# Two transformer blocks on one core: an expert weight ring that begins in the mixer's buffers, and a reordered head

## The chip, the cores and the metric

The kernel runs on one core of one Trainium2 chip, in one launch. The metric is the device time of that launch in microseconds, as a median of several runs. The engines are named as the profile names them: PE (TensorE, matrix multiplies), DVE (VectorE), ACT (ScalarE), POOL (GpSimd) and SP (SyncE, which here only issues DMAs).

## The reference

256 tokens of width 1024 (float32) and 256 context tokens go through two blocks.

```python
def adaln(cvec, w, b):                       # six vectors of 1024: shift, scale, gate, twice
    m = silu(cvec) @ w + b
    return split(m, 6)

# first block
x = x + sincos_2d(256)
hc = rms_norm(ctx, norm1_g) * (1 + csc1) + csh1
s_f, s_b = context_states(hc @ w_in[:, 512:2048])           # final states of gated linear attention
hx = rms_norm(x, norm1_g) * (1 + sc1) + sh1
x = x + gt1 * token_mixer(hx @ w_in, s_f, s_b)              # attention branch, convolution branch, merge
h = rms_norm(x, norm2_g) * (1 + sc2) + sh2
x = x + gt2 * hier_moe(h)        # 4 groups x 8 experts (1024 -> 512 -> 1024, gate and up), top 1 group, top 2 experts
x = rms_norm(x, final_norm_g)
# second block, two layers, each
hx, hc = modulate(rms_norm(x), adaln(c_2)), modulate(rms_norm(ctx_2), adaln(c_ctx_2))
# ... retention and gated linear attention over both, an MLP of 4096, each with a gate
```

All weights are float32 in HBM. The 32 experts alone are 201 MB (32 x 3 matrices of 1024 x 512).

## The kernel before, in words

The kernel is written in a tile framework: the program order sets priorities, a planner puts each engine's instructions into one fixed order by a cost model, and a tile's buffer is handed to the next tile of the same tag when its last reader is done. Each engine runs its own list in order. Weight loads all go through SP's one DMA queue, so a load that waits for its buffer holds back all loads behind it.

*Precision.* Most products are made from high and low halves: `split` (lines 204 to 217) loads a chunk of weights into a buffer "raw" (three in the pool `wp`), ACT rounds it into a "whi" buffer, DVE writes the rest into a "wlo" buffer (two of each), and `mm3` (lines 223 to 228) makes three matmuls.

*Head* (lines 551 to 580). `params_c` turns the two condition vectors into columns and applies silu. The shift of adaLN (columns 0 to 1023) is made on DVE by `ada`, with multiply-adds over 512 columns for both vectors (line 289). The scale (columns 1024 to 2047) is made on PE by `ada_pe`, with the vectors as the stationary operand, two output rows, and then transposes (lines 261 to 269). Both are generators and run in turns; each turn loads a 1 MB chunk, `ada` into the two "wlo" buffers, `ada_pe` into "raw". `params0` packs small parameters as rows of one tile `prow`, with DMAs that alternate between ACT's and SP's queues, and turns them. The context tokens are loaded at the third turn, transposed, and their sums of squares made on PE (`stats`, line 322). Then two chunks of `w_in` are split and the tokens x are loaded, transposed and summed. `norm_mod` writes the modulated, split activations `hh` and `hl` (lines 366 to 371), which the first projection (the values, lines 583 to 591) reads.

*Mixer* (lines 660 to 955). Chunks of 256 columns of `w_in` are projected by `proj`; between them `tick` runs pieces of the block's other adaLN vectors on DVE. `hg_pair` does two heads of the attention branch, twice; at each head it calls `next(pieces)`, one of the four pieces of the second block's adaLN shift (`ada_pe`, line 654). The filter of the convolution branch (`hyena_filter`) is issued on ACT after the instruction `early`, which is the square root of the context's statistics. The small loads of the router's weights (lines 858 to 864) go out on ACT's queue in the head.

*End of the mixer* (lines 956 to 1002). The tags h0 and h1 of the pool `xp` are free once the last projection has read `hh` and `hl`. Two loads of 2 MB go into them: the second block's adaLN scale (`adaw`). At the last chunk of `w_out` the first three expert chunks go into the "raw" buffers.

*Router and experts* (`moe`). `ada_pe` makes the second block's scale from `adaw` in pieces: one ahead of the router's chain on DVE, two ahead of the branch, the last ahead of the first experts. A branch (`tc.If(most > CAP)`, line 1163) guards a fallback for an expert with more than 64 tokens, which is not taken here. Expert weights come in 192 chunks of 1 MB through a ring of 14 buffers (`chunk`): three "raw" of `wp`, three "raw" of `pm`, two "whi", two "wlo", and four halves of h0 and h1. The first ten are loaded ahead of the branch, the four in h0 and h1 behind it. For each quad of experts tokens are gathered by matmuls with a selection tile (line 1234), then for pairs of experts come gate and up (line 1271), down (line 1301) and the weighted sum back (line 1319).

Of the kernel before, what the change touches and what calls it, by code (L numbers as in the profile page):

```python
# [26 lines left out]
def _consts():  # L27

    if CONSTS:
# [5 lines left out]
        [np.eye(P), np.tile((np.arange(24) == 15)[None], (P, 1)), np.tile(np.arange(8)[None], (P, 1))], 1).astype(f32)  # L35
# [87 lines left out]
class K:  # L123


    def __init__(self, nc, tc, I, out, cap=64, dbg=None):
# [13 lines left out]
        self.kres = self.cp.tile([P, 160], F32, name="kres")  # L140
        nc_.scalar.dma_start(self.kres, I["k_res"])
        self.ident = self.kres[:, 0:128]
        self.hot = self.kres[:, 128:160]
        self.ones = self.cp.tile([P, 256], F32, name="ones")
# [86 lines left out]
    def param_pack(self, i, rows, pool, eng):  # L231
# [14 lines left out]
    def ada_pe(self, pool, w, col0, s16, fin, got=()):  # L246

        nc = self.nc
        sv = s16.rearrange("p (i k) -> p k i", i=2)
        m = pool.tile([P, 16], F32, tag="adam", name="adam")  # L250
        for c in range(2):
            pt = self.mm()
            for q in range(2):
                if got:
                    v = got[c][:, 4 * q:4 * q + 4]
                else:
                    v = self.raw(w[512 * q:512 * q + 512, col0 + 512 * c:col0 + 512 * c + 512]
                                 .rearrange("(k p) c -> p k c", p=P))
                for kk in range(4):
                    k = 4 * q + kk  # L260
# [8 lines left out]
            nc.vector.tensor_copy(m.rearrange("p (i j) -> p j i", i=2)[:, 4 * c:4 * c + 4], p2[:, :, :2])  # L269
            yield  # L270
        fin(m)
# [128 lines left out]
def params_c(s, pool):  # L400
# [8 lines left out]
    nc.scalar.activation(s.sc, pt[:, :16], AF.Silu)  # L409


def params0(s, pool):
# [6 lines left out]
        (r(I["hy_d"][0]), 4), (r(I["hy_conv_b"][0]), 12)], pool, nc.scalar)  # L419
# [7 lines left out]
def params(s, pool):  # L427
# [10 lines left out]
    nc.scalar.activation(s.sc2, p1[:, 76:92], AF.Silu)  # L438
    s.cvw = p1[:, 0:36]
# [93 lines left out]
def block1_mixer(s):  # L533
    nc, tc, I = s.nc, s.tc, s.I
    mt = nc.tensor.matmul
    with tc.tile_pool(name="p1", bufs=1) as pool_:
        pool = Pool(pool_, {"b8": 5, "b4": 3, "s4": 4, "t2": 6, "sq": 3,
                            "etot": 2, "adam": 2},
                    {"rstd": "s4", "nt": "sq", "prow": "sqo", "adarow": "sqo"})
# [104 lines left out]
        pieces = s.ada_pe(pool, I["ada_w_2"][0], 0, s.sc2, fin0)  # L644
# [33 lines left out]
        def hg_pair(hp):  # L678
# [11 lines left out]
            for j in range(2):  # L690
                next(pieces, None)
# [166 lines left out]
        nc.scalar.dma_start(s.wr[:, :, 0:4], I["moe_router_g_w"][0].rearrange("(k p) g -> p k g", p=P))  # L858
        for g in range(4):
            nc.scalar.dma_start(s.wr[:, :, 4 + 8 * g:12 + 8 * g],  # L860
                                I["moe_router_e_w"][0, g].rearrange("(k p) e -> p k e", p=P))
        s.rb = s.cp.tile([P, 36], F32, name="rb")
        nc.scalar.dma_start(s.rb[:, 0:4], I["moe_router_g_b"].broadcast_to([P, 4]))
        nc.scalar.dma_start(s.rb[:, 4:36], I["moe_router_e_b"].rearrange("o g e -> o (g e)").broadcast_to([P, 32]))
# [91 lines left out]
        s.adaw = []  # L956
        for c in range(2):
            v = s.xp.tile([P, 8, 512], F32, tag=f"h{1 - c}", name="adaw")
# [1003 lines left out]
```

## Time and profile before

| | |
|---|---|
| time, median of 3 runs | 2000.6 us (2000.2 to 2002.79) |
| the profiled execution's own time | 2003.38 us |
| its span, first to last instruction | 2001.6 us |
| PE / DVE / ACT busy | 1925.4 / 1099.4 / 676.7 us |
| mean granted TensorE clock | 0.981 of full speed |
| moved by DMA | 426.18 MB, mean 213 GB/s |

The span can be read in stages: the head up to the first projection matmul, the mixer up to about 400 us, router and experts up to about 890 us, the second block up to the end. "Busy" of PE is modelled for pipelined matmuls, so a full PE can still be a slow one. A granted clock of 1.00 is 2.4 GHz, 0.50 is 1.2 GHz.

### The profile page before, as it was taken

Reading aid. Unit: us, or ns where it says so; the run is one execution under the profiler, and the core shown is the slowest. Engines: PE = TensorE matmul, PEld = TensorE weight load, DVE = VectorE, ACT = ScalarE, POOL = GpSimd, SP = SyncE. Lnnn points to the kernel's source line nnn. Section 1 sums busy time; section 2 is a strip of 40 time slices with the busy share of each in tenths; the row PEclk is TensorE's granted clock in tenths of the full one; section 3 lists DMA queues with packets and bytes.
Section 4 is the critical chain, followed back from the end, with each engine's and each line's share of the span. In section 5 each row is a group of like instructions: output and inputs, shape, how many; then the busy total and the mean of one; then the engine's idle time right before and its main releaser. Section 6 shows DMA issues by size and latency. Waiting matters only on the chain.

```text
span 2001.6 us, 28164 instructions
## 1 busy us (share of the span) xinstructions
PE 1925.4 (96%) x11748; PEld 1438.7 (72%) x11748; DVE 1099.4 (55%) x2034; ACT 676.7 (34%) x991; POOL 6.1 (0%) x18
## 2 busy tenths in 40 slices
PE   6998999999999999989999999999999999999998
PEld 2856679944444444448888888778788968989998
DVE  5768796531111111125869858565534656887555
ACT  2564544421111111033432333231323444443444
POOL 0000000000000000000000000000000000000000
PEclk8999999999999999989999999999999989989999
DMA  8535537889999999973243523444323244457552
GB/s 282 174 107 192 167 127 239 288 356 421 421 421 421 421 421 421 421 271 110 67 147 127 170 64 128 152 141 147 126 84 106 56 137 148 157 180 232 187 176 101
DMA packets 217882, 426.18 MB, mean 213 GB/s; under 512 B 16171, under 2 KB 152392, under 8 KB 192920
## 3 DMA queue, kind: packets, MB, share of 16 engines
q1 hardware_dynamic: 208616, 419.75, 57.8%
q10 hardware_dynamic: 9008, 4.51, 0.8%
q8 instruction: 94, 1.54, 0.3%
q14 instruction: 36, 0.29, 0.0%
q0 software_dynamic: 128, 0.08, 0.0%
HBM read 423.26 MB, written 1.05 MB: 212 GB/s over the span
## 4 chain that ended last, share of the span: by engine, by line
PE 68%; DVE 4%; DMA 4%; ACT 2%; issue 0%; DVEq 0%; ACTq 0%; SPq 0%
PE mm L226 14%; PE mm L228 14%; PE mm L227 14%; PE mm L1271 10%; PE mm L1301 3%; PE at L1301 3%; DMA raw<-in_moe_w_down_dram 2%; PE at L1234 2%; PE at L1319 1%; PE tr L296 1%; DVE wlo L216 1%; DMA raw<-in_moe_w_up_dram 1%; DMA rawh<-in_moe_w_gate_dram 1%; DVE acc L289 1%; ACT whi L215 1%; PE at L1712 1%
## 5 line engine op out<-in xcount | busy, mean ns | idle before, releaser
L226 PE MATMUL mm<-hh,whi 128*128 128x256 f32 (+2 forms) x1232 | 411.4, 334 | 6.0 <-DVE sq L1890 2.4
L228 PE MATMUL mm<-hh,wlo 128*128 128x256 f32 (+2 forms) x1232 | 406.1, 330 | 8.7 <-DVE wlo L216 8.7
L227 PE MATMUL mm<-hl,whi 128*128 128x256 f32 (+2 forms) x1232 | 408.1, 331 | 0.1
L216 DVE TENSOR_TENSOR wlo<-raw,whi 128x2048 fp32r<-128x2048 f32 (+2 forms) x138 | 303.6, 2200 | 179.2 <-ACT whi L215 178.9
L215 ACT CAST whi<-raw 128x2048 fp32r<-128x2048 f32 (+2 forms) x138 | 253.1, 1834 | 359.5 <-PE mm L227 317.8
L226 PEld LDWEIGHTS mm<-hh,whi 128*128 128x128 f32 (+1 forms) x1232 | 236.2, 192 | 33.8 <-issue 5.0
L228 PEld LDWEIGHTS mm<-hh,wlo 128*128 128x128 f32 (+1 forms) x1232 | 236.2, 192 | 32.9 <-DVE wlo L216 10.0
L227 PEld LDWEIGHTS mm<-hl,whi 128*128 128x128 f32 (+1 forms) x1232 | 236.0, 192 | 25.4 <-issue 5.5
L289 DVE SCALAR_TENSOR_TENSOR acc<-raw,sc,acc 128x512 f32<-128x512 f32 x308 | 219.2, 744 | 15.3 <-DMA raw<-in_ada_w_dram 13.9
L226 PE MATMUL mm<-hidh,whi 128*128 128x256 f32 (+1 forms) x544 | 178.9, 331 | 0.0
L228 PE MATMUL mm<-hidh,wlo 128*128 128x256 f32 (+1 forms) x544 | 177.4, 329 | 0.1
L227 PE MATMUL mm<-hidl,whi 128*128 128x256 f32 (+1 forms) x544 | 177.2, 328 | 0.0
L1271 PE MATMUL mm<-raw,xg 128*64 128x512 f32 x736 | 172.5, 595 | 1.0 <-DMA raw<-in_moe_w_up_dram 1.0
L228 PE MATMUL mm<-whi,hl 128*128 128x256 f32 x512 | 148.6, 291 | 2.8 <-DVE hl L371 2.8
L226 PE MATMUL mm<-whi,hh 128*128 128x256 f32 x512 | 149.0, 292 | 2.2 <-ACT hh L370 1.3
L227 PE MATMUL mm<-wlo,hh 128*128 128x256 f32 x512 | 147.6, 288 | 0.0
L1271 PEld LDWEIGHTS mm<-raw,xg 128*64 128x64 f32 x736 | 54.6, 137 | 97.7 <-issue 93.0
L1279 DVE SCALAR_TENSOR_TENSOR glo<-mm,ws,glo 128x512 f32<-128x512 f32 x16 | 12.0, 751 | 190.2 <-PE mm L1271 168.2
L228 PEld LDWEIGHTS mm<-hidh,wlo 128*128 128x128 f32 x544 | 102.0, 188 | 11.2 <-DVE wlo L216 0.7
L227 PEld LDWEIGHTS mm<-hidl,whi 128*128 128x128 f32 x544 | 102.1, 188 | 11.0 <-DVE hidl L221 0.8
L226 PEld LDWEIGHTS mm<-hidh,whi 128*128 128x128 f32 x544 | 101.7, 188 | 10.8 <-ACT hidh L220 0.9
L226 PEld LDWEIGHTS mm<-whi,hh 128*128 128x128 f32 x512 | 99.3, 194 | 5.6 <-issue 2.8
(504 smaller groups left out, 2650.6 us busy)
## 6 DMA issues: line engine op xcount, KB each, us to landing
raw<-in_ada_w_dram SPq DMA_DIRECT2D x68, 1024.0 KB, 5.5
raw<-in_w_mlp_dram SPq DMA_DIRECT2D x64, 1024.0 KB, 5.4
raw<-in_w_in_dram SPq DMA_DIRECT2D x48, 1024.0 KB, 5.3
raw<-in_moe_w_down_dram SPq DMA_DIRECT2D x48, 1024.0 KB, 16.4
raw<-in_moe_w_gate_dram SPq DMA_DIRECT2D x46, 1024.0 KB, 13.1
raw<-in_moe_w_up_dram SPq DMA_DIRECT2D x46, 1024.0 KB, 15.0
rawh<-in_moe_w_gate_dram SPq DMA_DIRECT2D x18, 1024.0 KB, 12.8
rawh<-in_moe_w_up_dram SPq DMA_DIRECT2D x18, 1024.0 KB, 11.6
```

What stands on the lines that cost most here:

```text
L215: self.nc.scalar.copy(hv, v)
L216: self.nc.vector.tensor_tensor(lv, v, hv, op=OP.subtract)
L226: mt(out, ah, bh, start=first, stop=False)
L227: mt(out, ah, bl, start=False, stop=False)
L228: mt(out, al, bh, start=False, stop=last)
L289: nc.vector.scalar_tensor_tensor(acc[:, i], v[:, kk], s[:, k:k + 1], acc[:, i], op0=OP.mult, op1=OP.add)
L296: nc.tensor.matmul(pt[:n, :P], self.hot[:, 15 - r:15 - r + n], acc[:, r // 4, (r % 4) * P:(r % 4 + 1) * P], start=r == 0, stop=r == n - 1)
L1234: mt(px, tk[:, a, k * P:(k + 1) * P], sel[:, a], start=tk is th and a == 0, stop=tk is tl and a == 1)
L1271: mt(pg[64 * j:64 * j + 64], xg[:, k, 2 * i + j], vs[j][:, kk], start=k == 0, stop=k == 7)
L1301: mt(pd[c][sl], hT[:, k, sl], vs[j][:, kk, 512 * c:512 * c + 512], start=k == 0, stop=k == 3)
L1319: mt(po[:, j], y[:, i, sl], selT[:, i], start=y is yh and i == 0, stop=y is yl and i == 1)
L1712: mt(po[:, 2 * g + t], sc[:, a, t * P:(t + 1) * P], vr[:, 2 * g + a, h * P:(h + 1) * P], start=a == 0, stop=g == 1 and a == 1)
```

## The change

1. Head: both halves of the first adaLN are made by `ada_pe`. The context tokens are loaded ahead of all weights, x after the first pair of chunks; transposes and statistics of both, and the split of the first chunk of `w_in`, are in the loop over the turns. The parameter rows all go out on POOL's queue. `early` is now the last ACT instruction of the context's modulation, and the router's small loads are issued after it.
2. `ada_pe`: the stationary operand is a tile `sw` of 32 columns for each k, zero but for the two vectors; the four k of a chunk write four groups of 32 PSUM rows. The row copy takes all 128 rows, and a matmul with `pick2` turns and sums them.
3. The second block's adaLN scale is made in the mixer, behind its shift: 8 pieces, two at each head.
4. The h0 and h1 buffers take the first four expert chunks where `adaw` was loaded. The ring begins there, and all 14 chunks are issued ahead of the branch. The fallback's tile `h32` moves to another tag.

```diff
+         p[:, None] % 32 == np.arange(2)[None]], 1).astype(f32)      # pick2, in k_res
 def param_pack(self, i, rows, pool, eng):
-            (eng, self.nc.sync)[j % 2].dma_start(t[o:o + r], ap)
+            eng.dma_start(t[o:o + r], ap)
-    def ada_pe(self, pool, w, col0, s16, fin, got=()):
+    def ada_pe(self, pool, w, col0, s32, fin, got=(), src=()):
...
-                    nc.tensor.matmul(pt[:2], sv[:, k], v[:, kk], start=k == 0, stop=k == 7)
+                    nc.tensor.matmul(pt[32 * kk:32 * kk + 32], s32[:, 4 * q + kk], v[:, kk], start=q == 0, stop=q == 1)
                 if q == 0:
                     yield
-            row = pool.tile([2, 512], F32, name="adarow2")
-            nc.scalar.copy(row, pt[:2])
+            row = pool.tile([P, 512], F32, tag="adarow2", name="adarow2")
+            nc.scalar.copy(row, pt)
             p2 = self.tr((P, 4, 128))
             for j in range(4):
-                nc.tensor.transpose(p2[:, j, :2], row[:, j * P:(j + 1) * P], self.ident[:2, :2])
+                nc.tensor.matmul(p2[:, j, :2], row[:, j * P:(j + 1) * P], self.pick2, start=True, stop=True)
...
+    s.sw = pool.tile([P, 8, 32], F32, name="sw")
+    nc.vector.memset(s.sw, 0.0)
+    nc.vector.tensor_copy(s.sw[:, :, 0:2], s.sc.rearrange("p (i k) -> p k i", i=2))
...
+        tcx = s.load(pool, I["ctx"][0])
-        both = [s.ada(pool, ada, 0, [sx, s.sc[:, 8:16]], fin0, "s4", (s.wp, "wlo")), s.ada_pe(pool, ada, 1024, s.sc, fin1)]
+        both = [s.ada_pe(pool, ada, 0, s.sw, fin0, src=(s.wp, "wlo")), s.ada_pe(pool, ada, 1024, s.sw, fin1)]
+        wv = []
         for i in range(5):
             for g in both:
                 next(g, None)
             if i == 0:
-                params0(s, pool)
-            if i == 2:
-                tcx = s.load(pool, I["ctx"][0])
+                tx = s.load(pool, I["x"][0])
                 s.to_T(tcx, ctxT)
                 rc = s.stats(pool, ctxT, T)
-        early = s.sqrt
-        wv = [s.split(w_in[:, :, 1536:1792])]
-        tx = s.load(pool, I["x"][0])
+            if i == 1:
+                params0(s, pool)
+                s.to_T(tx, s.xT, pos=pos)
+                rx = s.stats(pool, s.xT, T)
+                wv.append(s.split(w_in[:, :, 1536:1792]))
+        s.norm_mod(pool, ctxT, md["Ac"], md["Bc"], hh[:, :, T:], hl[:, :, T:], r=rc)
+        early = s.act
         wv.append(s.split(w_in[:, :, 1792:2048]))
-        s.norm_mod(pool, ctxT, md["Ac"], md["Bc"], hh[:, :, T:], hl[:, :, T:], r=rc)
-        s.to_T(tx, s.xT, pos=pos)
-        rx = s.stats(pool, s.xT, T)
...
-        pieces = s.ada_pe(pool, I["ada_w_2"][0], 0, s.sc2, fin0)
+        pieces = chain(*(s.ada_pe(pool, I["ada_w_2"][0], 1024 * i, s.sw2, f) for i, f in enumerate((fin0, fin1))))
...
             for j in range(2):
+                next(pieces, None)
                 next(pieces, None)
...
-        for c in range(2):
-            v = s.xp.tile([P, 8, 512], F32, tag=f"h{1 - c}", name="adaw")
-            nc.sync.dma_start(v, I["ada_w_2"][0][:, 1024 + 512 * c:1536 + 512 * c].rearrange("(k p) c -> p k c", p=P))
-            s.adaw.append(v)
+        s.big = [s.xp.tile([P, 2, 2048], F32, tag=f"h{1 - h}", name="rawh") for h in range(2)]
+        s.pre = []
+        for i in range(4):
+            src = s.expert_w(0, i // 2, i % 2)
+            v = s.big[i // 2][:, i % 2].rearrange("p (k c) -> p k c", k=src.shape[1])
+            nc.sync.dma_start(v, src)
+            s.pre.append(v)
...
-                s.pre = [s.raw(s.expert_w(0, i // 2, i % 2)) for i in range(3)]
+                s.pre += [s.raw(s.expert_w(0, i // 2, i % 2)) for i in range(4, 7)]
...
-        with tc.issue_after(s.turned):
-            next(pieces)
-        for _ in range(2):
-            next(pieces)
-        pre = s.pre + [chunk(i) for i in range(3, len(slots))]
-        made = len(slots)
+        made = len(slots) + 4
+        pre = s.pre + [chunk(i) for i in range(len(s.pre), made)]
-        todo += [lambda: list(pieces)]
```

## Rows read from the trace of the kernel before

**Rows 1.** The profile page: busy us of each engine over the span

```profile
PE 1925.4 (96%) x11748; PEld 1438.7 (72%) x11748; DVE 1099.4 (55%) x2034; ACT 676.7 (34%) x991; POOL 6.1 (0%) x18
```

**Rows 2.** Windows of the head: engines' busy us, granted clock, DMA share, GB/s

```profile
10.00:20.00 10.00, 6.41 (x9) 1.01 (x9) 3.76 (x6) 0.00 (x0) 0.00 (x0) 0.98 0.52 127
20.00:30.00 10.00, 5.87 (x11) 1.29 (x12) 7.36 (x15) 0.00 (x0) 0.00 (x0) 0.51 1.05 398
60.00:70.00 10.00, 10.00 (x70) 9.58 (x70) 4.74 (x12) 6.92 (x16) 0.00 (x0) 0.97 0.40 132
```

**Rows 3.** Timeline of the head, SP's queue, then POOL: start us, length, what

```profile
1.20 1.92 SPq L175 DMA_DIRECT2D raw<-in_ada_w_dram  x2
...
11.30 0.29 SPq L239 DMA_DIRECT2D prow<-in_norm_g_dram  x1
...
27.08 0.92 SPq L175 DMA_DIRECT2D raw<-in_ada_w_dram  x2
...
50.28 0.51 POOL L239 DMA_DIRECT2D prow<-in_c_dram  x1
```

**Rows 4.** Timeline of ACT, DVE and PE up to the first projection matmul

```profile
49.13 0.57 ACT L265 COPY adarow<-mm 2x512 f32<-2x512 f32 x1 [2.83 <-PE mm L261]
...
52.34 0.16 DVE L457 SCALAR_TENSOR_TENSOR mAc<-mAc,par 128x8 f32<-128x8 f32 x1
...
53.02 2.28 DVE L216 TENSOR_TENSOR wlo<-raw,whi 128x2048 fp32r<-128x2048 f32 x1
55.22 1.27 DVE L366 SCALAR_TENSOR_TENSOR nt<-ctxT,mAc,rstd 128x256 f32<-128x256 f32 x3
...
56.29 0.39 PE L226 MATMUL at<-whi,hh 128*128 128x256 f32 x1 [3.23 <-ACT hh L370]
```

**Rows 5.** A window of the mixer

```profile
160.00:170.00 10.00, 7.96 (x44) 5.40 (x42) 9.47 (x26) 4.28 (x7) 0.00 (x0) 1.00 0.17 64
```

**Rows 6.** Windows of the experts

```profile
416.00:794.00 378.00, 377.13 (x1884) 166.97 (x1886) 57.74 (x153) 58.32 (x131) 0.00 (x0) 1.00 1.01 419
822.00:876.00 54.00, 50.46 (x226) 19.93 (x224) 7.77 (x14) 5.99 (x9) 0.00 (x0) 1.00 1.01 418
```

**Rows 7.** The chain of waits at the experts' end: start us, us, what

```profile
855.66 19.84 DMA raw<-in_moe_w_down_dram
```

**Rows 8.** The page's DMA issues: count, KB each, us from issue to landing

```profile
raw<-in_ada_w_dram SPq DMA_DIRECT2D x68, 1024.0 KB, 5.5
```

**Rows 9.** Instruction groups, 0 to 84 us: count, busy us, mean ns, idle

```profile
L322 PE MATMUL mm<-sq,ones 128*128 128x256 f32 x32 | 7.8, 382 | 0.6 <-ACT sq L321 0.6
```

**Rows 10.** Groups of instructions, 84 to 400 us

```profile
L261 PE MATMUL mm<-raw,sc 128*2 128x512 f32 x32 | 14.9, 592 | 0.0
L787 PE MATMUL po<-states,b 128*32 128x128 f32 x128 | 5.3, 279 | 0.0
```

**Rows 11.** Timeline of the router, DVE, then PE

```profile
408.12 0.17 DVE L1071 TENSOR_SCALAR w<-dd 128x2 f32<-128x2 f32 x1 [1.43 <-ACT dd L1067]
...
412.54 2.52 DVE L1220 TENSOR_SCALAR sel<-km,rank 128x64 fp32r<-128x64 f32 x15
...
411.54 4.45 PE L261 MATMUL mm<-adaw,sc 128*2 128x512 f32 x10
416.37 0.48 PE L1234 MATMUL at<-sel,th 128*128 128x256 f32 x2 [0.38 <-PEq L1163]
```

**Rows 12.** Windows of the router

```profile
400.00:402.00 2.00, 2.00 (x3) 0.25 (x2) 1.90 (x10) 0.85 (x3) 0.00 (x0) 0.53 0.89 219
402.00:404.00 2.00, 2.00 (x6) 0.43 (x5) 2.00 (x9) 1.71 (x4) 0.00 (x0) 1.00 1.02 422
```

**Rows 13.** Timeline of SP's queue around the branch

```profile
354.90 2.48 SPq L959 DMA_DIRECT2D adaw<-in_ada_w_dram  x2
...
416.02 1.70 SPq L1148 DMA_DIRECT2D rawh<-in_moe_w_gate_dram  x2
...
425.22 0.80 SPq L1148 DMA_DIRECT2D raw<-in_moe_w_up_dram  x2
```

More of the change, by code (lines that the diff above doesn't have):

```diff
@@ L1 @@
 import math
+from itertools import chain
 from contextlib import ExitStack
@@ L139, in __init__ @@
         nc_ = nc
-        self.kres = self.cp.tile([P, 160], F32, name="kres")
+        self.kres = self.cp.tile([P, 162], F32, name="kres")
         nc_.scalar.dma_start(self.kres, I["k_res"])
@@ L143, in __init__ @@
         self.hot = self.kres[:, 128:160]
+        self.pick2 = self.kres[:, 160:162]
         self.ones = self.cp.tile([P, 256], F32, name="ones")
@@ L438, in params @@
     nc.scalar.activation(s.sc2, p1[:, 76:92], AF.Silu)
+    s.sw2 = s.sw
+    nc.vector.tensor_copy(s.sw2[:, :, 0:2], s.sc2.rearrange("p (i k) -> p k i", i=2))
     s.cvw = p1[:, 0:36]
@@ L643, in block1_mixer, with fin1 @@
         s.bg = [s.ada(pool, ada, 1024 * (i + 2), [sx], f) for i, f in enumerate((fin2, fin3, fin4, fin5))]
-        pieces = s.ada_pe(pool, I["ada_w_2"][0], 0, s.sc2, fin0)
+        def fin1(m):
+            s.md2 += [fin_scale(s, m, 8 * i, s.adab2[0][:, 8:16], s.n1g2[0], f"mA{i}") for i in range(2)]
+        pieces = chain(*(s.ada_pe(pool, I["ada_w_2"][0], 1024 * i, s.sw2, f) for i, f in enumerate((fin0, fin1))))
         def proj(c0, n, act=None):
@@ L857, in block1_mixer @@
         s.wr = s.cp.tile([P, 8, 36], F32, name="wr")
[L858 to L861, printed above, removed]
         s.rb = s.cp.tile([P, 36], F32, name="rb")
-        nc.scalar.dma_start(s.rb[:, 0:4], I["moe_router_g_b"].broadcast_to([P, 4]))
-        nc.scalar.dma_start(s.rb[:, 4:36], I["moe_router_e_b"].rearrange("o g e -> o (g e)").broadcast_to([P, 32]))
+        with tc.issue_after(early):
+            nc.scalar.dma_start(s.wr[:, :, 0:4], I["moe_router_g_w"][0].rearrange("(k p) g -> p k g", p=P))
+            for g in range(4):
+                nc.scalar.dma_start(s.wr[:, :, 4 + 8 * g:12 + 8 * g],
+                                    I["moe_router_e_w"][0, g].rearrange("(k p) e -> p k e", p=P))
+            nc.scalar.dma_start(s.rb[:, 0:4], I["moe_router_g_b"].broadcast_to([P, 4]))
+            nc.scalar.dma_start(s.rb[:, 4:36], I["moe_router_e_b"].rearrange("o g e -> o (g e)").broadcast_to([P, 32]))
         ybT = b8([P, 2, 4, T], F32R, name="ybT")
@@ L1011, in moe @@
                     {"nt": "sq", "adarow2": "glo"})
-        bias = s.adab2[0]
-        def fin1(m):
-            s.md2 += [fin_scale(s, m, 8 * i, bias[:, 8:16], s.n1g2[0], f"mA{i}") for i in range(2)]
-        pieces = s.ada_pe(pool, I["ada_w_2"][0], 1024, s.sc2, fin1, s.adaw)
         cols = s.cols
@@ L1133, in moe @@
         slots = [(s.wp, "raw")] * 3 + [(pool, "raw")] * 3 + [(s.wp, "whi"), (s.wp, "wlo")] * 2
-        big = []
         def chunk(i):
             n = i % (len(slots) + 4)
-            if n < len(slots):
-                p_, tag = slots[n]
+            if n < 4:
+                t = s.big[n // 2][:, n % 2]
+            else:
+                p_, tag = slots[n - 4]
                 t = p_.tile([P, 2048], F32, tag=tag, name="raw")
-            else:
-                if len(big) < 2:
-                    big.extend(s.xp.tile([P, 2, 2048], F32, tag=f"h{h}", name="rawh") for h in range(2))
-                t = big[(n - len(slots)) // 2][:, n % 2]
             src = s.expert_w(*order[i])
@@ L1163, in moe @@
         with tc.If(most > CAP):
-            h32 = s.xp.tile([P, 8, T], F32, tag="h1", name="h32")
+            h32 = pool.tile([P, 8, T], F32, tag="xg", name="h32")
             s.norm_mod(pool, s.xT, s.A2, s.B2, h32=h32, r=s.rows(pool, cols))
```

14 lines of the change are left out of this document (6 added, 8 removed).

## The prediction

> **What bounds the kernel now.** I read the page first: TensorE (PE) is busy for 96% of the span [rows 1], so what can be won are stretches where PE waits, or work on PE that is done twice as cheaply. Then I read windows along the three places that the diff touches. In the head, before the first projection matmul, PE is busy but the loads set the pace: the memory moves 127 GB/s from 10 to 20 us and 398 GB/s right behind [rows 2]. The timeline of SP says why: two weight chunks go out at 1.20, then the queue stands until 11.30 at a row of the parameter pack, and the last two adaLN chunks are issued only at 27.08 [rows 3]. From their results to the first projection matmul the timelines of ACT, DVE and PE give a chain: adaLN row copied at 49.13, scale ready at 52.34, a weight split on DVE at 53.02, first matmul at 56.29 [rows 4]. From 60 us on PE is full [rows 2]. In the mixer PE is mostly full, with short stretches that DVE sets [rows 5]. The experts run at 419 GB/s throughout, PE idle for 3.5 of 54 us near their end [rows 6], and the chain of waits ends there in a weight load [rows 7]: the experts are bound by PE and memory nearly equally.
>
> **The head.** Removed: the DVE form of the first adaLN half (its sums now run on PE), the SP rows of the parameter pack, the router's small loads on ACT's queue. Moved: ctx goes first on SP, x follows the first pair of adaLN chunks, both are transposed and their statistics made while adaLN weights still land. Up to the last adaLN chunk SP now issues ctx, x, eight adaLN chunks and one of w_in: 11 loads of 1024 KB [rows 8], 11.53 MB, none of them behind a parameter row. At 398 GB/s [rows 2] they take 29.0 us. One such load lands 5.5 us after its issue [rows 8], of which 2.6 are its bytes, so 2.9 us lie around a stream: it ends at 1.20 + 2.9 + 29.0 = 33.1. Behind it come eight instructions of the last quarter sums (about 1 us by the prices below, at the low clock), then from the row copy to the scale 52.34 - 49.13 plus its end, 3.4, and from the first modulated tile to the first matmul about 1.1, the split of 2.28 us [rows 4] no longer between, because that chunk has landed earlier. The first projection matmul then starts at 38.6 in place of 56.29 [rows 4]: 17.7 us. The sums of squares on PE, 7.8 us for ctx and x together [rows 9], were half (x) inside the full stretch and now lie ahead of it: 3.9 more. Head: 21.6 us.
>
> Its bounds. Higher rate: at the 419 GB/s of [rows 6] the stream is 1.5 us shorter, and without the 2.9 us the gain is 26. Lower: a "wlo" buffer is taken by the split of the first w_in chunk, so that the last two chunks of the first half pass through one buffer, costs one landing, 5.5; 5 us of the stream at the 127 GB/s of [rows 2] cost 3 to 4 more: 12. Below nothing is excluded here: the whole of the removed wait lies ahead of the full PE. The parameter rows all go to POOL's queue: one issue takes 0.51 us there [rows 3], seven take 3.6, and they are wanted 25 us later, so nothing; POOL has no other work there. Were they late, every microsecond would count in full. The moved router loads are first read by the router's matmuls behind the mixer, so nothing either.
>
> **The mixer.** The scale of the second block's adaLN is made here instead of in the router: 4 more chunks through the three raw buffers (8 pieces, where 4 were), and each piece's matmuls write four 32-row groups of PSUM, so that four can run side by side. Before: 32 instructions in 14.9 us [rows 10], 0.466 each. After: 64. No row shows four groups at 512 columns; the nearest is the state readout (line 787, 32 rows out, 128 columns): 128 in 5.3 us [rows 10], 0.041 each, so 0.166 for 512 columns, 10.6 us for 64. Without any overlap it is 29.8, with a perfect one 7.5. I take the row: 4.3 us less on PE. By the Trainium skill ("TensorE: Matmul & The Clock Gate", Part 3, on packing small matmuls) three column tiles gave 2.38 times, which carried on to four is an estimate of 9.4 us in place of 10.6; no run here shows that yet. Of the 4.3 I count half, 2, as in the windows of [rows 5] DVE and not PE is full. The bounds are -15 and +7. The four loads cost nothing by [rows 5], 64 GB/s in a window where 419 is possible; behind them on SP stand the projection weights, and these would be late if a piece held its buffer. The quarters are summed by the small matmul with `pick2`, which takes the place of the transposes one for one.
>
> **Router and experts.** The last pieces leave the router. Two places on its path gain. DVE waits 1.43 us for an exponential that stood behind the copy of an adaLN row on ACT [rows 11]. PE does ten piece instructions from 411.54 to 416.0, and the first gather follows at 416.37 [rows 11], although the selection that it reads was ready at 412.54 + 2.52 = 415.06 [rows 11]. Without both the gather starts at about 415.06 - 1.43 + 0.1 = 413.7: 2.6 earlier. But PE will then have stood nearly still since 399. What that does, the window of 400 to 402 shows: granted clock 0.53, after PE had just begun on pieces, and 1.00 from 402 [rows 12], so half speed for about 4 us, 2 us lost. By the Trainium skill ("TensorE: Matmul & The Clock Gate", Part 1) the throttled clock is the default and activity releases it: by that rule the removed pieces were what held the clock up, and the row agrees. Net 0.6, between 2.6 and -0.1 (a whole slow window like 20 to 30 us, clock 0.51 [rows 2], costs a little more).
>
> The ring: the 2 x 2 MB of adaLN at 354.90 [rows 13] become four expert chunks of the same size, so nothing behind them on SP moves. Before, 10 chunks are out ahead of the branch, four more go out from 416.02, and the first freed buffer is refilled at 425.22 [rows 13]. After, all 14 have landed by then, but memory has nothing to do until that same first refill. Of its four chunks the old ring has landed about three by 425. So the new one is only one chunk ahead, 1.0486 MB at 419 GB/s [rows 6], 2.5 us, and not four chunks, 10 us. The 3.5 us of PE's idle time near the end [rows 6] can take 2.5. Experts and router: 3.1, between 0 and 6.1.
>
> **Sum.** 21.6 + 2 + 3.1 = 26.7 us off a profiled execution with a span of 2001.6 us, which itself took 2003.38 and lies 2.8 above the median of 2000.6. From the median: 1973.9, forecast **1974 us**. What the measurement of this kernel can tell from no change is about 0.2%, 4 us.
>
> **Rivals.** *The mixer does not hand it on.* The filter's loads are issued on ACT behind `early`, which moves from a square root ahead of the modulation to the last ACT instruction of ctx's modulation, so in absolute time hardly earlier; and DVE-bound windows [rows 5] may close up. For: 9.47 of 10 us DVE there. Against: PE is full from 60 to 70 [rows 2] and all these engines start earlier together. Half the head's gain: 2000.6 - 10.8 - 5.1 = 1985.
>
> *No overlap in the four groups.* 14.9 us more on PE in the mixer instead of 2 less: 2000.6 - 21.6 - 3.1 + 14.9 = 1991. Against: 0.041 us per instruction [rows 10] is not possible one after another, when 512 columns take 0.466.
>
> *Slower: pieces stall PE.* PE takes its matmuls in order; if each of the 8 pieces stands ahead of its own load, PE waits one landing of 5.5 us [rows 8] each time, 44 us: 2000.6 - 24.7 + 44 = 2020. It decides from 24.7 / 8 = 3.1 us a piece. For: twice as many pieces on the same three buffers. Against: PE is idle for 0.0 us ahead of the mixer's pieces now [rows 10].
>
> *The head does not do what it says*, because buffers and not the parameter rows held SP: 2000.6 - 5.1 = 1995.5, or no change with a small loss elsewhere. Against: the queue's standstill ends at a parameter row [rows 3].
>
> *Everything at its better bound:* head 26, mixer 7, experts 6: 1962.
>
> **How the numbers follow.** Forecast 0.55 (own range 1966 to 1981), mixer swallows half 0.17, no overlap 0.08, head fails 0.08, slower 0.05, better bound 0.07. 1963 to 1991 leaves out the slower case, the failed head and half of the best one, under 2 in 10. Faster by over 0.2%: all but the slower case and about half of the failed head, 0.91; within: 0.04; slower: 0.05.
>
> **What would show it.** Head: memory at about 390 GB/s without a hole from 3 to 33 us, first projection matmul at 36 to 42, no DVE multiply-adds of adaLN ahead of it. Mixer: 64 pieces' instructions in 8 to 14 us, no wait for an adaLN load ahead of them. Router: no piece between 399 and the first gather (times less the shift), clock about 0.5 over the first gathers. Ring: 14 chunks issued ahead of the branch, then a hole in memory traffic of over 10 us up to the first refill, and PE's waits for weights near the end down to about 1 us. The prediction is wrong if the first matmul comes after 46, or if PE waits in the mixer for adaLN loads.

## The result, and the profile after

The changed kernel takes 2011.99 us (median of 5 runs, 2009.4 to 2014.64) against 2000.6 for the kernel before, measured beside it: a ratio of 1.0054, interval 1.0043 to 1.0065. It is 11 us slower, where 1974 was forecast. Its profiled execution took 2012.78 us, with a span of 2011.0.

The page has PE at about the same share as before [rows 1], over a longer span:

```profile
PE 1914.9 (95%) x11786; PEld 1451.2 (72%) x11786; DVE 1080.4 (54%) x2003; ACT 676.2 (34%) x991; POOL 11.0 (1%) x28
```

Windows of the kernel after, with the columns of [rows 2]; first the head, then the mixer:

```profile
10.00:20.00 10.00, 10.00 (x48) 5.04 (x47) 0.00 (x0) 5.38 (x11) 0.00 (x0) 1.00 1.04 388
20.00:30.00 10.00, 8.26 (x51) 6.24 (x48) 6.20 (x13) 4.80 (x9) 3.00 (x6) 0.83 1.06 376
40.00:50.00 10.00, 7.47 (x35) 5.79 (x28) 6.52 (x18) 2.87 (x7) 0.00 (x0) 0.50 0.78 266
...
130.00:140.00 10.00, 7.95 (x39) 4.75 (x32) 9.19 (x22) 6.55 (x7) 0.00 (x0) 0.93 0.86 280
160.00:170.00 10.00, 6.22 (x21) 3.86 (x19) 9.04 (x19) 1.69 (x3) 0.00 (x0) 0.79 0.49 167
180.00:190.00 10.00, 6.91 (x35) 6.16 (x36) 9.08 (x17) 3.02 (x6) 0.00 (x0) 0.66 0.62 210
```

The stream of the head is there: 388 GB/s where there were 127 [rows 2]. In the mixer PE now has holes, and the granted clock is lower: 0.79 from 160 to 170 us, where [rows 5] had 1.00. SP's queue in the head, for [rows 3], and PE's timeline, for [rows 4]:

```profile
1.20 0.42 SPq L379 DMA_DIRECT2D xtok<-in_ctx_dram  x1
...
3.49 3.68 SPq L178 DMA_DIRECT2D raw<-in_ada_w_dram  x2
...
15.65 8.38 SPq L178 DMA_DIRECT2D raw<-in_ada_w_dram  x3
31.44 0.37 SPq L178 DMA_DIRECT2D raw<-in_w_in_dram  x1
34.15 0.37 SPq L178 DMA_DIRECT2D raw<-in_ada_w_dram  x1
```

```profile
39.66 1.93 PE L263 MATMUL mm<-raw,sw 128*32 128x512 f32 x8 [3.85 <-DMA raw<-in_ada_w_dram]
42.29 3.57 PE L270 MATMUL tr<-kres,adarow 128*128 128x2 f32 x16 [0.70 <-ACT adarow L267]
47.70 0.58 PE L229 MATMUL mm<-whi,hh 128*128 128x256 f32 x1 [1.83 <-ACT hh L373]
```

The last adaLN chunk is issued only at 34.15, behind a `w_in` chunk that waited until 31.44. The view of SP's waits from 0 to 40 us names the split of the first `w_in` chunk:

```profile
SPq L178 <- DVE wlo L219: 7.3, 1, 7.3
```

PE waits 3.85 us for the landing of the last adaLN chunk, and the first projection matmul comes at 47.70 (forecast 38.6, before 56.29).

To see where time goes I compare the start of the same instruction in two profiled executions (start in the run minus start before, us). *Values*: last copy of `vt` (84.4 before). *Conv*: first convolution tile `u` (165.3). *Filter*: first product with the filter's inverse transform, `pc` (205.7). *w_out*: last residual sum of `xT` (394.7). *Silu*: first silu of the experts (429.2). *Norm*: the block's final scale `fa` (897.7). The last column is the median against that of the kernel before, measured beside it. The stages come from one execution of each kernel, and the executions of one kernel lie 2 to 7 us apart, so a difference of 1 or 2 us between two rows shows little.

| run | values | conv | filter | w_out | silu | norm | median, us | against before |
|---|---|---|---|---|---|---|---|---|
| after | -11.3 | 0.0 | +2.4 | +10.1 | +11.0 | +10.7 | 2011.99 | +11.4 |
| e1 | -11.8 | -2.1 | -4.0 | -4.0 | -1.2 | -0.7 | 1999.34 | -1.6 |
| e2 | -2.4 | +9.0 | +11.2 | +17.1 | +16.4 | +17.7 | 2015.99 | +15.0 |
| e3 | -11.8 | -0.6 | +1.5 | +6.6 | +8.3 | +8.5 | 2011.72 | +10.8 |
| e4 | -0.1 | +11.3 | +13.4 | +21.2 | +22.0 | +20.4 | 2024.85 | +23.9 |
| e5 | -11.6 | -3.4 | -4.0 | +1.6 | +3.0 | +2.8 | 2005.0 | +3.4 |
| e6 | -14.1 | -2.6 | -2.5 | +8.0 | +8.7 | +8.5 | 2008.95 | +7.3 |
| e7 | -6.7 | -6.3 | -5.5 | -5.7 | -7.3 | -7.3 | 1997.48 | -4.2 |
| e8 | -14.3 | -11.1 | -11.3 | -5.6 | -3.8 | -3.5 | 1998.32 | -3.3 |
| **e9** | -14.3 | -12.0 | -12.1 | -12.2 | -12.5 | -12.5 | **1992.31** | **-9.9** |
| e10 | -14.1 | -6.5 | -6.5 | -8.1 | -8.0 | -9.7 | 1996.02 | -6.2 |
| e11 | -15.3 | -10.6 | -11.2 | -7.0 | -7.0 | -7.4 | 1995.13 | -7.1 |
| e12 | -1.3 | +0.2 | +1.2 | +1.2 | +3.3 | +2.4 | 2004.79 | +2.6 |
| e13 | -13.9 | -8.6 | -9.2 | -11.3 | -9.4 | -8.5 | 1991.0 | -11.1 |
| e14 | -13.8 | -10.6 | -10.8 | +0.7 | +1.2 | +0.5 | 2002.43 | +0.4 |
| e15 | -15.0 | -12.3 | -12.4 | -12.4 | -11.5 | -11.7 | 1991.99 | -10.1 |

The kernel after is 11.3 us ahead when the values are done and 10.1 behind at the end of the mixer: the mixer loses 21.4. Router, experts and second block change little more. The runs e3, e11, e13 and e15 leave the second block's scale at its bias, so their result is not the reference's; they only separate costs.

### The profile page after: what moved, and what is told of

Its sections match the earlier page's. It is cut to its first block, busy times and chain, and to the rows that moved or that the text cites. A ratio compares the mean times of both kernels' runs of the same rounds, so it can differ in the third digit from the quotient of the medians.

```text
span 2011.0 us, 28248 instructions
## 1 busy us (share of the span) xinstructions
PE 1914.9 (95%) x11786; PEld 1451.2 (72%) x11786; DVE 1080.4 (54%) x2003; ACT 676.2 (34%) x991; POOL 11.0 (1%) x28
## 4 chain that ended last, share of the span: by engine, by line
PE 68%; DVE 4%; DMA 4%; ACT 2%; issue 0%; DVEq 0%; ACTq 0%; SPq 0%
PE mm L229 14%; PE mm L231 14%; PE mm L230 14%; PE mm L1272 10%; PE mm L1302 3%; PE at L1302 3%; DMA raw<-in_moe_w_down_dram 2%; PE at L1235 2%; PE at L1320 1%; PE tr L299 1%; DMA rawh<-in_moe_w_up_dram 1%; DVE wlo L219 1%; DMA raw<-in_moe_w_gate_dram 1%; DVE acc L292 1%; ACT whi L218 1%; PE at L1712 1%
## 5 line engine op out<-in xcount | busy, mean ns | idle before, releaser
L231 PE MATMUL mm<-hh,wlo 128*128 128x256 f32 (+2 forms) x1232 | 411.6, 335 | 7.6 <-DVE wlo L219 7.4
L230 PE MATMUL mm<-hl,whi 128*128 128x256 f32 (+2 forms) x1232 | 412.3, 335 | 0.3 <-DVE hl L374 0.3
L231 PEld LDWEIGHTS mm<-hh,wlo 128*128 128x128 f32 (+1 forms) x1232 | 239.1, 194 | 32.6 <-DVE wlo L219 10.1
L292 DVE SCALAR_TENSOR_TENSOR acc<-raw,sc,acc 128x512 f32<-128x512 f32 x280 | 200.2, 745 | 10.6 <-DMA raw<-in_ada_w_dram 9.1
## 6 DMA issues: line engine op xcount, KB each, us to landing
raw<-in_moe_w_gate_dram SPq DMA_DIRECT2D x44, 1024.0 KB, 16.4
rawh<-in_moe_w_gate_dram SPq DMA_DIRECT2D x20, 1024.0 KB, 14.1
```

The costliest lines, as they stand in the source:

```text
L230: mt(out, ah, bl, start=False, stop=False)
L231: mt(out, al, bh, start=False, stop=last)
L292: nc.vector.scalar_tensor_tensor(acc[:, i], v[:, kk], s[:, k:k + 1], acc[:, i], op0=OP.mult, op1=OP.add)
```

## The experiments

**e1: the head alone; e2: the mixer and the ring alone.**

```diff
 e1: as after, but
+        pieces = s.ada_pe(pool, I["ada_w_2"][0], 0, s.sw2, fin0)     # shift only, one piece per head
+            nc.sync.dma_start(v, I["ada_w_2"][0][...])               # adaw, scale in the router, old ring
 e2: as after, but the head (order of loads, rows on SP, ada for the shift, router loads) of before
```

> The new head and the quarters as they are after the change; the scale of the second block is made in the router and the ring begins as before the change (no extra piece loads in the mixer; the tile of the vectors lies in the constant pool). Three theories of where the head's 11 us went. W (weight queue): the four extra 1 MB piece loads stand ahead of projection weights in SP's queue and cost the mixer some 20 us; then this kernel keeps the head's gain, 1985 to 1992, with the last merge of the mixer 8 to 11 us earlier than before the change. A (ACT's queue): the small loads that now stand behind ctx's modulation hold the first weight splits, 8 us between the values (73.1) and the first sigmoid (97.5); then 1995 to 2000. D (swallowed): stretches set by DVE close up whatever arrives earlier; then 1999 to 2002.

> The head of before the change (order of loads, parameter rows, router's small loads), with the eight pieces in the mixer, the quarters and the new ring. W: the extra loads alone cost, 2008 to 2016. A: no loss, as nothing of ACT's queue has moved: 1996 to 2001. D: between, about 2001 to 2004 with the clock at the first gathers (2 to 4 us) as the only loss.

The ratios are 0.9989 (0.998 to 0.9998) and 1.0081 (1.0067 to 1.0095). The mixer's part costs 15 us by itself, so A is no sufficient account; but the head alone keeps only 4 us of 11.8, which speaks against W alone.

**e3: no extra loads; e4: ACT's queue as before.**

```diff
 e3
-        pieces = chain(*(s.ada_pe(..., s.sw2, f) for ...))
+        pieces = chain(*(s.ada_pe(..., s.sw2, f, ([hh.bitcast(F32)] * 2 if i else ())) for ...))
 e4
-        early = s.act                     # behind ctx's modulation
+                early = s.sqrt            # ctx's statistics
-        with tc.issue_after(early):       # router's small loads: unconditioned again
```

> The kernel after, but the four pieces of the scale (both heads of the second pair) read the resident activations in place of weights, and the scale is then set to its bias alone: the same matmuls on PE, four loads of 1 MB fewer, the first pair of heads unchanged. W: nothing changes up to the convolution (first u at 165.3), and of the 8 us that the second pair and the gates lose (from +2.4 to +10.8) most comes back: 2003 to 2007. A and D: 2010 to 2013.

> The kernel after, with the router's small loads unconditioned on ACT's queue as before the change, and the filter's loads behind ctx's square root as before. A: the split for the first gate projection no longer shares ACT with them; first sigmoid near 90 in place of 97.5 and the time 2002 to 2006. W: the first sigmoid may be earlier, but the next projection's weights stay at about 124 behind five piece loads: 2009 to 2013. D: the same, 2009 to 2013.

e3 stays at 2011.72, ratio 1.0048 (1.0034 to 1.0062): W as stated falls, though w_out comes 3.5 us earlier than after. e4 contradicts A outright, and W and D did not expect it either: 2024.85, ratio 1.0121 (1.0105 to 1.0136). Nearly the whole loss against after lies in the head (values -0.1), and SP's queue in e4 shows where it begins:

```profile
2.76 8.47 SPq L178 DMA_DIRECT2D raw<-in_ada_w_dram  x2
11.43 0.37 SPq L379 DMA_DIRECT2D xtok<-in_x_dram  x1
```

No parameter row stands on SP any more, yet the queue stands until 11.43, as it did before the change until 11.30 [rows 3]. What is back in the front is the router's small loads. Further back e4's other edit counts too: in the view of SP's waits from 0 to 40 us one of the filter's small loads, issued earlier now, holds SP for 6.0 us, so the loss is not all the router's.

```profile
SPq L178 <- DMA fb<-in_hy_filt_freq_dram: 6.0, 1, 6.0
```

**e5: rows of the pieces in another tag; e6: split of the first `w_in` chunk behind the last adaLN piece; e8: both.**

```diff
 e5, e8
-                    {..., "adarow": "sqo", "adarow2": "t2"})
+                    {..., "adarow": "sqo", "adarow2": "b4"})
 e6, e8
-                wv.append(s.split(w_in[:, :, 1536:1792]))      # in the turns, i == 1
+        wv.append(s.split(w_in[:, :, 1536:1792]))              # behind the turns
```

> The kernel after with one word changed: the row copies of the pieces take buffers of the tag b4, which the attention heads hardly use, and not of t2, whose six buffers carry the heads' tiles (e, kt, b, de, ket, vm, dr, qm, km). Theory T (the rows share the heads' buffers): a row that waits for its weights stands ahead of the head's own tiles in the order in which buffers are handed out; so the first scan of a head waits for a piece, and that costs the mixer most of what it lost: ctx's modulation as in the kernel after, first convolution tile near 157 to 161 in place of 165.3, time 1996 to 2004. Theory P (the pieces' matmuls, their PSUM tiles and copies are what costs): 2009 to 2013. W, four loads more in SP's queue, has lost most of its ground by the run without these loads and would also give 2009 to 2013.

> The kernel after, with the split of the first chunk of w_in behind the last adaLN piece in place of between the turns, so that both wlo buffers are left to the adaLN chunks. Head: the last adaLN chunk is issued at 24 to 28 in place of 34.15, and the first projection matmul comes at 42 to 45 in place of 47.70 (the split of 4 us then lies partly on the path). If the mixer hands that on (H): 2006 to 2009. If it swallows it (D): 2010 to 2013.

> Both edits on the kernel after: rows in b4 and the split behind the last piece. T and H: first projection matmul at 42 to 45, last merge of the mixer 5 to 14 us earlier than before the change, 1989 to 1998. T alone: 1996 to 2004. P and D: 2008 to 2013.

e5: ratio 1.0019 (1.001 to 1.0028), 8 us under after by one word (+3.4 against +11.4; T had expected up to 2004). DVE's timeline of the kernel after, then of e5, shows a scan that is held back:

```profile
113.36 0.48 DVE L710 TENSOR_SCALAR sm<-sm,oml 128x512 f32<-128x512 f32 x1
...
122.00 0.69 DVE L701 COPY q<-mm 128x512 f32<-128x512 f32 x1 [0.16 <-PE mm L231]
122.62 0.68 DVE L717 TENSOR_TENSOR_SCAN e<-ones,sg 128x255 f32<-128x255 f32 x1
```

```profile
114.83 0.68 DVE L719 TENSOR_TENSOR_SCAN e<-ones,sg 128x255 f32<-128x255 f32 x1
...
121.75 0.69 DVE L701 COPY q<-mm 128x512 f32<-128x512 f32 x1 [0.17 <-PE mm L231]
```

In the kernel after both scans of the first head stand behind `q`, from 122.62; in e5, where `e` shares its tag with no piece, the second one starts at 114.83. But little of these 8 us gets through: the copy of `kt` behind them starts at 127.94 in the kernel after and at 127.23 in e5. ACT's longest wait for `e` is at the second head, in the kernel after, then in e5:

```profile
146.66 0.63 ACT L721 ACTIVATE e<-e 128x512 f32<-128x512 f32 x1 [7.92 <-DVE e L719]
```

```profile
143.13 0.63 ACT L721 ACTIVATE e<-e 128x512 f32<-128x512 f32 x1 [2.83 <-DVE e L719]
```

The 3.5 us between these two starts are what the convolution gains (3.4). In both runs DVE makes the scans of the second head right behind the copy of a piece's result (144.92 and 141.42), and ahead of that copy it waits for PE, 2.81 us in the kernel after and 0.26 in e5. PE's order differs there too. So the cost of the word is shown; how much of it is a wait for buffers and how much the other order is not.

e6, ratio 1.004 (1.0026 to 1.0053), brings the values 2.8 us earlier than in after, and 2.1 of it reach w_out even while the rows stay in t2, as H had it. e8, ratio 0.9987 (0.9978 to 0.9996), has its first projection matmul at 43.15 and keeps 11.3 us up to the filter. From there to w_out 5.7 are still lost, and 1998.32 lies just outside what T and H had given (1989 to 1998).

**e7: the kernel before, with only the router's small loads moved.**

```diff
+        with tc.issue_after(early):
             nc.scalar.dma_start(s.wr[:, :, 0:4], ...)          # and the six behind it
```

> The kernel before the change, with the router's small loads (seven, in short rows) behind the same instruction as the filter's loads, and nothing else. Theory R: it is these loads, 6720 short rows that the DMA engines work off from 1 to 12 us, and not the parameter rows on SP, that held SP's queue until 11.3; then the third and fourth adaLN chunk go out at about 4 to 6 us in place of 13.18, the first projection matmul comes 6 to 9 us earlier (47 to 50), and the time is 1992 to 1997, if the mixer hands it on. The reading of the prediction (the rows hold SP): SP stands until 11.3 as before, 1999 to 2002.

Ratio 0.9981 (0.9972 to 0.999), 4.2 us under before, in the lower half of the gain that R gave. (The expectation's count of 6720 rows was wrong.) That the loads hold SP can be read in the kernel before itself, where a parameter row waits for one of them (SP's waits, 0 to 40 us):

```profile
SPq L239 <- DMA wr<-in_moe_router_e_w_dram: 8.0, 1, 8.0
```

The DMA view of the first 15 us, of before and of e7, counts the packets; they differ by 5228 under 512 bytes:

```profile
DMA packets 6803, 2.54 MB, mean 169 GB/s; under 512 B 5397, under 2 KB 5773, under 8 KB 6803
```

```profile
DMA packets 2192, 3.66 MB, mean 244 GB/s; under 512 B 169, under 2 KB 545, under 8 KB 2192
```

These loads also hold ACT: the silu of the condition vectors, which all adaLN needs, in before and in e7:

```profile
2.69 4.68 ACTq L860 DMA_DIRECT2D wr<-in_moe_router_e_w_dram  x2
...
8.69 0.18 ACT L409 ACTIVATE sc<-tr 128x16 f32<-128x16 f32 x1
```

```profile
3.57 0.18 ACT L409 ACTIVATE sc<-tr 128x16 f32<-128x16 f32 x1
```

But R is only half of it. The parameter rows stay on SP in e7, and its next adaLN chunks go out at 10.00 us, not at 4 to 6:

```profile
10.00 2.61 SPq L175 DMA_DIRECT2D raw<-in_ada_w_dram  x4
```

SP's early standstill shortens by 3 us only. The third chunk goes out at 13.18 with rows and loads (before), at 10.00 with the rows alone (e7), at 12.21 with the loads alone (e4), and at 3.49 with neither (after, in another order of loads). So the queue stands with either of the two, and moves only without both. The 6.7 us that the values gain reach w_out as 5.7: the mixer of the kernel before does hand on what it gets.

**e9: head of the change, mended, with the second block's adaLN and the ring as before; e10: the same with quarters.**

```diff
 e9: as e8, but
+        pieces = s.ada_pe2(pool, I["ada_w_2"][0], 0, s.sc2, fin0)          # two output rows, as before
+        pieces = s.ada_pe2(pool, I["ada_w_2"][0], 1024, s.sc2, fin1, s.adaw)   # in the router
 e10: both with ada_pe and sw2 (four groups; sw in the constant pool)
```

> Only the head of the change, with its two mends (rows of the pieces in b4, the split of the first chunk of w_in behind the last adaLN piece); the second block's adaLN is as before the change, with the same two-row form, the shift in the mixer (four pieces) and the scale in the router, and the ring begins as before. If the mixer hands on what the head gives once its heads wait for nothing of the pieces, all stages from the first sigmoid on are 9 to 13 us earlier: 1988 to 1993. If the mixer swallows part of every earlier start by itself: 1994 to 1999.

> The kernel of the run e9 with one difference: the second block's adaLN pieces, in the mixer and in the router, have the form with four groups of rows. Theory C (clock): in the router the old form keeps PE busy until the first gather; the new one leaves it idle, the granted clock is 0.5 over the first gathers, and 2 to 4 us are lost from there: first silu of the experts later by 2 to 3 us against the router's begin than in e9, time 2 to 4 us more than e9. Rival: the router's chain is DVE's and the shorter pieces help by up to 2 us: 0 to 2 us less than e9.

e9 beats both kernels: 1992.31 us, ratio 0.9954 (0.9941 to 0.9968). From the convolution on everything is 12 us earlier. e10 has 0.9972 (0.9962 to 0.9982). Windows of the router, of e9 and then e10, show the clock as C has it; from the count of the selection (`mxi`) to the first silu e10 loses 1.9 us, e9 0.2:

```profile
402.00:406.00 4.00, 3.62 (x21) 2.20 (x19) 0.40 (x3) 1.50 (x4) 0.00 (x0) 1.00 0.39 84
406.00:410.00 4.00, 4.00 (x43) 3.28 (x44) 0.90 (x7) 2.62 (x7) 0.00 (x0) 1.00 0.99 399
```

```profile
402.00:406.00 4.00, 0.90 (x5) 0.76 (x4) 3.03 (x19) 0.00 (x0) 0.00 (x0) 0.50 0.54 158
406.00:410.00 4.00, 3.39 (x18) 3.42 (x19) 0.44 (x3) 1.12 (x3) 0.00 (x0) 0.57 0.97 393
```

But most of the difference arises in the mixer, which C did not foresee: with pieces that cost PE 5.3 us in place of 14.9, the convolution comes 5.5 us later. In e10's window from 120 to 130 us PE is busy for 3.92 of 10, at a clock of 0.63; PE waits once for 5.8 us on DVE's `de`, which waits on ACT. ACT's order differs there: e10 has the logarithm `sg` of the second head, with a table load of 1.28 us ahead of it, between `etot` and `de`, and `de` starts at 125.05, in e9 at 123.34. So with the other form of the pieces came another order of the heads.

**e11: the scale's pieces cut to their loads; e13: their work without the loads; e14: moved into the merge.**

```diff
 e11: as e8, but of each chunk one matmul
+                mt(pt[:32, :128], s.sw2[:, 0], v[:, 0, :128], start=True, stop=True)
 e13: e8 with the pieces' operand of e3
 e14: as e8, but
-                next(pieces, None); next(pieces, None)          # at the heads of the second pair
+                next(pieces)                                    # behind each pair of gates in the merge
```

> The kernel of the run e8 with the second pair's scale pieces cut to their loads: of each 1 MB chunk one matmul of 128 columns remains, the rest of the matmuls, the row copies and the small matmuls are left out, and the scale is set from its bias alone. The run without the loads kept a loss of 5 us in the second pair. Theory P (the pieces' own work on PE, its PSUM tiles and copies are what costs there): the last gate is 4 to 7 us earlier than in e8, time 1991 to 1995. Rival (planning, or the loads after all): 1997 to 2000 as e8.

> The kernel of the run e8 (rows in b4, split behind), but the scale's pieces read the resident activations in place of four loads, and the scale is its bias alone. In e8 the mixer lost 5.7 us between the convolution and w_out, and with the loads alone (e11) still 4.3. If the loads are the cause (W in a new form: the four loads go ahead of the block's own adaLN chunks in SP's queue, and their multiply-adds on DVE fall into the stretch in which DVE is full): w_out 9 to 11 us earlier than before the change, against 5.6 in e8, time 1993 to 1995. If the pieces' work on PE and ACT is: as e8, 1997 to 2000.

> The kernel of the run e8 with the four scale pieces moved from the second pair of heads into the merge stage, one behind each pair of gates, where PE is full and DVE is not. If their place among DVE's full stretches was the cost: 5 us saved, of which their matmuls and small matmuls (about 7 us of PE by the rows of the kernel after) are paid again: 1997 to 2000. If PE takes them in gaps: 1993 to 1996. If the loads delay the merge's weights: above 2000.

Against before: e11 0.9969 (0.9959 to 0.9979), e13 0.9941 (0.9927 to 0.9955), e14 1.0003 (0.9994 to 1.0012). At w_out the pieces' own work is worth 1.4 us (e11 against e8), the loads 5.7 (e13 against e8). The medians, each against its own before, put them at 3.8 and 7.8; e11's 1995.13 lies at the edge of what P gave. So the loads are the larger part and W comes back in another form, but P is not excluded for the rest. The windows of DVE's multiply-adds (tile `acc`) of e8, then of e13:

```profile
220.00:240.00 20.00, 0.00 (x0) 1.00 0.63 210
240.00:260.00 20.00, 4.15 (x6) 1.00 0.44 144
260.00:280.00 20.00, 4.02 (x7) 0.83 0.51 161
```

```profile
220.00:240.00 20.00, 4.23 (x6) 1.00 0.49 159
240.00:260.00 20.00, 1.49 (x2) 1.00 0.31 106
260.00:280.00 20.00, 1.97 (x3) 1.00 0.17 53
```

In e8 four adaLN chunks fill SP's queue at a stretch:

```profile
201.98 23.84 SPq L178 DMA_DIRECT2D raw<-in_ada_w_dram  x4
```

The block's own adaLN chunks come behind them, so no multiply-add falls between 220 and 240 us, where DVE is busy for 11.18 of 20, and 13 fall between 240 and 280, where it has 39.0 of 40 to do. From 220 to 280 PE is idle for 7.5 us in e8 and for 3.4 in e13. e3, with its rows still in t2, had shown 3.5 us of it at w_out. The merge is no better place (e14): the scale's pieces take 7.3 us of PE there (5.3 and 2.0), PE waits 3.5 us for the halves of splits, and w_out comes 11.5 us later than the filter had promised.

**e12: the kernel before with its piece rows in t2; e15: the new ring without the scale's cost.**

```diff
 e12, on the kernel before
+                    {..., "adarow": "sqo", "adarow2": "t2"})
 e15: as e8, but four shift pieces of two rows, one per head, and no scale pieces
```

> The kernel before the change with one word changed: the row copies of its four shift pieces (and of the head's scale pieces) take buffers of the tag t2. Theory T by itself: two rows in the mixer where the kernel after has four: first convolution tile and all behind it 2 to 6 us later, time 2003 to 2007. Rival (the rows hurt only where two pieces stand at one head): 2000 to 2002.

> The mixer and head of the run e9, with the ring of the kernel after (begun in h0 and h1, all 14 chunks ahead of the branch), and with the second block's scale left out altogether (its bias alone), so that the ring and the empty router are seen free of charge. The prediction's terms: 2.6 us from the shorter router, 2.5 from the ring, 2 lost to the clock: 3 us less than e9, 1988 to 1990. Rival: the half clock over the first gathers delays the first freed buffer, memory stands idle until then, and ring and router together give nothing or lose: 1992 to 1995.

e12: ratio 1.0015 (1.0005 to 1.0024). Its time, 2004.79, is the one that T gave, but not the place: the first convolution tile is 0.2 us later, not 2 to 6, and w_out 1.2. Another 2.1 appear between w_out and the first silu. There PE stands for 1.81 us between two gathers, for no wait that the profile shows, and the granted clock behind it is 0.50 from 422 to 424 us, where before had 1.00:

```profile
422.07 0.37 PE L1234 MATMUL at<-sel,th 128*128 128x256 f32 x1 [1.81 <-issue]
```

So T by itself is not shown; with two pieces at each head the same word costs 8.5 at w_out. e15: 0.9956 (0.9942 to 0.9969), as e9, with the scale left out altogether. SP's queue in e9, then in e15, at the branch, and e15's window behind it:

```profile
403.36 1.70 SPq L1181 DMA_DIRECT2D rawh<-in_moe_w_gate_dram  x2
405.18 1.07 SPq L1181 DMA_DIRECT2D rawh<-in_moe_w_up_dram  x2
412.71 0.80 SPq L1181 DMA_DIRECT2D raw<-in_moe_w_up_dram  x2
```

```profile
398.15 0.33 SPq L1178 DMA_DIRECT2D raw<-in_moe_w_up_dram  x1
412.89 0.81 SPq L1178 DMA_DIRECT2D rawh<-in_moe_w_up_dram  x2
```

```profile
406.00:410.00 4.00, 4.00 (x39) 3.41 (x40) 0.71 (x5) 2.61 (x7) 0.00 (x0) 0.90 0.02 4
810.00:864.00 54.00, 51.57 (x227) 20.31 (x224) 7.77 (x14) 5.99 (x9) 0.00 (x0) 1.00 1.01 418
```

Both refill the ring for the first time at the same moment, and the new ring's memory stands still until then (4 GB/s): the rival of e15's expectation.

## Why the prediction was wrong, by its own steps

**The head, 21.6 forecast: 11.3 measured, and partly for another reason.** "None of them behind a parameter row" named one of two causes. By the view of waits the row at which the standstill ended was itself held by one of the router's small loads, which were costed at nothing; moved alone they bring the values 6.7 us earlier (e7), and e4, which brings them back, has none of the head's gain left. By the Trainium skill ("DMA: Bandwidth & Descriptors", section "Bandwidth") transfers under 64 KB are dominated by their descriptors; these are of 2 to 32 KB, and the packets in e7 agree. The stream then broke at the step that the lower bound named, a wlo buffer taken by the first split: the last chunk is issued at 34.15 and not in the stream. Without that the values come 14.3 us earlier (e8). The first projection is then still at 43.15, since the split that was "no longer between" lies on the path in that version. The chain behind the stream was too short as well: from the last landing to the first projection matmul 5.5 us were summed, and the kernel after takes 8.0 (39.66 to 47.70). `pick2` does not replace the transposes "one for one": the two last row copies are followed by 16 instructions in 3.57 us, at a granted clock of 0.50, where before one row had 4 in 0.41. The prediction's own sign of being wrong, a first matmul after 46, came (47.70).

**The mixer, 2 us of gain forecast: 21.4 of loss.** The size of the pieces' large matmuls was right, 9.8 us for 64 where 10.6 were taken from [rows 10]; that of the small ones with `pick2` was put at nothing:

```profile
L263 PE MATMUL mm<-raw,sw 128*32 128x512 f32 x64 | 9.8, 601 | 0.0
L270 PE MATMUL tr<-kres,adarow 128*128 128x2 f32 x32 | 4.2, 254 | 2.2 <-ACT adarow L267 2.2
```

By the Trainium skill ("TensorE: Matmul & The Clock Gate", Part 3) the estimate had been 9.4; the measured row lies between the two. The transposes before took 0.8 us (8), the small matmuls take 4.2, so PE saves 1.7 us on the pieces and not 4.3. But PE's time was not what mattered: the prediction's signs for the mixer (64 pieces in 8 to 14 us, no wait ahead of them) held, and the mixer lost 21.4 all the same. From the values to w_out the kernel after loses 21.4, e5 13.2, e8 8.7, e13 2.6. The rows in t2: 8.2 (after against e5). The prediction did not cost that word of the change at all. The split's place: 4.5 (e5 against e8), beside 2.7 in the head; with the rows in t2 the same edit makes no such difference in the mixer (e6 loses 22.1), so the parts depend on their order. The four loads: 6.1 (e8 against e13). "Cost nothing by 64 GB/s" judged them by memory's bandwidth; what they took was their place in SP's order and in three buffers. What came late, by the windows of e8 and e13, was not the projections' weights but DVE's background work, which landed where DVE was full; no run tests that route by itself. The 2.6 that are left are lost without the scale's pieces too (2.1 in e9, 2.6 in e15). These parts add up to 21.4 by construction, as each is the difference of two neighbours in a row of runs.

**The rivals.** *Mixer does not hand it on* was right that part of the gain goes, but not that an early start is swallowed: e7 and e9 pass on 5.7 of 6.7 and 12.2 of 14.3. *Pieces stall PE* had the sign, not the place: PE waits 0.0 us ahead of their large matmuls and 2.2 us, for ACT, ahead of the small ones. *No overlap* falls with the 9.8 us.

**Router and experts, 3.1 forecast: a loss of about 1, even for free (e15).** e15 is 12.6 us ahead at the router's begin and 14.8 at the selection's count, but only 14.1 at the first gather (416.37 before [rows 11]):

```profile
402.27 1.17 PE L1264 MATMUL at<-sel,th 128*128 128x256 f32 x4
```

So 1.5 are gained up to there, where 2.6 were forecast. The clock's part is too small: between the first gather and the first silu 2.6 are lost, not 2. In the kernel after the two are 1.3 and 2.1, and its windows of the router and of the first gathers show the clock:

```profile
410.00:412.00 2.00, 0.00 (x0) 0.00 (x0) 1.90 (x11) 0.92 (x4) 0.00 (x0) 0.50 0.83 204
...
426.00:428.00 2.00, 2.00 (x11) 2.00 (x11) 0.00 (x0) 0.74 (x2) 0.00 (x0) 0.50 0.00 0
428.00:430.00 2.00, 2.00 (x19) 1.93 (x19) 0.00 (x0) 1.21 (x4) 0.00 (x0) 0.83 0.00 0
```

From 410 us PE does hardly anything, and the first gathers run at 1.2 GHz. Of the ring's 2.5 hardly anything arrives: PE is idle for 2.4 of 54 us near the end in e15, against 3.5 [rows 6], but from the first silu to the block's end only 0.2 are gained (-11.5 to -11.7). That is 1.5 - 2.6 + 0.2 = -0.9.

**What stays open.** How far each loss in the mixer is a wait and how far the planner's other order can't be separated: in e10 5.5 us go with another order, though its pieces cost PE less. The 2.3 us that e9 loses between values and convolution, and why PE pauses at e12's gathers, were not followed up.

## What to carry to other kernels

Read every word of a change that gives a tile another tag: a row that waits for a load and shares a ring of buffers with the tiles of the critical chain can delay them, and changing one word was worth 8.5 us at the mixer's end. A load is not free because memory is idle: in an in-order queue ask what stands behind it, and whether the engine that gets its work later then still has room. Before moving work out of a gap, as the pieces out of the router, ask what it did there: it filled PE's idle time, and with it gone the granted clock was 0.50 over the first gathers.

## What was not expected of the hardware

Seven small loads with some 5200 packets under 512 bytes, 162 KB in all (four of 32 KB, two of 16, one of 2), cost the head of the kernel before 6.7 us: ACT's issue of two of them took 4.68 us, and the silu behind came at 8.69 instead of 3.57. Short pauses of PE can cost more than their length, as the clock falls with them: in the kernel after, the window in which PE was idle for 3.8 of 10 us (160 to 170) has a granted clock of 0.79, and that from 180 to 190, with 3.1 idle, 0.66, while [rows 5], with 2.0 idle, stood at 1.00.
